# Transposes of the attention between single products of the projections instead of in runs

## The chip, the core and the metric

The kernel runs on one core of a Trainium2 chip. The metric is the time of one execution on the device, in microseconds (us). A core has a matrix engine (TensorE, PE in the profile, with its weight loads as PEld), three engines for elementwise work (VectorE or DVE, ScalarE or ACT, GpSimd or POOL) and a queue that issues transfers (SyncE or SP).

## The reference

One layer of a trunk for 512 tokens of width 1024, all in fp32. Three groups of attention heads share one input projection and one output projection; a gated MLP with a short convolution and a gated per-layer input follow.

```python
hn = rms_norm(h, ln_mix)
z = hn @ w_in                       # 1024 x 3590
(q1, q2, k1, k2, va, qf, kf, vf, fg, qc, kc, vc) = jnp.split(z, IN_SPLITS, axis=-1)
# A: differential attention, 4 heads:  softmax(q1 k1 + bias) - lam * softmax(q2 k2 + bias)
# B: forgetting attention, 6 heads:    bias from F = cumsum(log_sigmoid(fg + fgate_bias))
# C: chunked attention, 6 heads:       clipped relative-position bias
# q and k are RMS-normed for each head, head size 64
h = h + jnp.concatenate([o_a, o_b, o_c], axis=-1) @ w_out
h = h + conv_gated_mlp(rms_norm(h, ln_ffn), w_up, conv_w, conv_b, w_down)
gate = jax.nn.sigmoid(rms_norm(h, ln_ple) @ w_ple_gate)
h = h + (p @ w_ple_proj) * gate
```

## The kernel before

**Products.** Every fp32 operand is split into a high and a low part, and a product of two of them is three matmuls: high x high, high x low and low x high (`mm3`). A projection of 128 tokens has eight groups of three, one for each 128 rows of the weights; they add up in one PSUM bank, z. The columns are those of a pair of heads: `A0`, `A0b`, `A1`, `A1b` (two maps of two pairs of heads of A), `B0` to `B2`, `C0` to `C2`. For pairs of B and C, 384 columns are the q, k and v of two heads. The output projection (`wo`) has six groups of 512 columns.

**Attention.** For each pair of heads q and k come out of the projection with tokens in the partitions (`zn`). Four transposes for q and four for k (`feature_cols`, names `q_p` and `k_p`) put features in the partitions; ACT and DVE then split the results (`q_q`, `ql`, `k_k`, `kl`), and POOL moves halves together. Scores (`s`) follow, then the softmax on DVE, ACT and POOL (`e` and `st`). The probabilities are transposed as well (`prob_cols`): a run of four (`pt`), a run of three (`pt`) and a run of three (`ptc`) for each head; ACT and DVE split each (`pth`, `ptl`, `ptc`), and the products with the values (`po`) follow. `forget_cumsum` transposes the gates of B (`pf`), adds them up along the tokens with a scan on DVE (`fs`) and transposes the sums back (`pq`). A transpose is a matmul with a 128 x 128 identity as the moving operand (`ident` in the rows), in fp32. Its results go to one of three PSUM banks with the tag t; the z banks are two, and so are those for scores.

**Order of the work.** All of TensorE's order is written out by hand (`pe.pinned`). One slot is the projection of 128 tokens, or one block of the output projection. `run` goes through the eight groups of a slot, and behind each it lets one step of the attention issue its work: at first those that the table `T` names for this slot, from the group given there on. What is left at the slot's end is issued there in one go. A step issues one run of transposes, or one block of scores, or a pair of products with the values:

```python
for j in range(8):
    next(fill, None)
    while todo and j >= todo[0][0]:
        try:
            step(*todo[0][1:])
            break
        except StopIteration:
            todo.pop(0)
```

So before, a run of four transposes stands behind the third matmul of a group and ahead of the next group. On the attention's other engines the order isn't pinned: the scheduler of the framework sets it by priority (which follows the order in which the code issues the work, with the shifts of `EARLY`) and by its own model of time, when the program is built. Each engine then works in that order.

Nearly all instructions go through one recording helper, so they have the line L104 in the profile; they are told apart by their tiles. The rows leave out buffer numbers, and names of pairs are shortened: `A_`, `B_` and `C_` stand for any pair of the group. `B_l<-B_r,B_h` is a split of weights loaded ahead for a later projection.

Of the kernel before, what the change touches and what calls it, by code (L numbers as in the profile page):

```python
# [15 lines left out]
P = 128  # L16
D = 1024
S = 512
NT = S // P
KD = D // P  # L20
# [12 lines left out]
C_MIX, C_QK, C_SUB, C_CONV0, C_CONV1, C_CONV2, C_PLE, C_CONVB, C_FFN, C_FGB, C_LAM, NSMALL = (  # L33
    0, 8, 14, 16, 60, 104, 148, 156, 200, 208, 214, 470)
# [43 lines left out]
def kernel(ctx: ExitStack, tc: tile.TileContext, x, xt0, xt, pt_in, small, bias_c,  # L78
# [33 lines left out]
    pe, act, dve, pool, sp = (Engine(e) for e in (nc.tensor, nc.scalar, nc.vector, nc.gpsimd, nc.sync))  # L112
# [10 lines left out]
    Th = [cp.tile([P, 4, S], F32R, tag=f"Th{g}", name=f"Th{g}") for g in range(2)]  # L123
    Tl = [cp.tile([P, 4, S], F32R, tag=f"Tl{g}", name=f"Tl{g}") for g in range(2)]
# [12 lines left out]
    ident = cp.tile([P, P], F32, tag="ident", name="ident")  # L137
# [95 lines left out]
    def load_rect(w, k0, nk, c0, ncol, name, eng=dve, gain=None):  # L233
        rows = w[k0 * P : (k0 + nk) * P, c0 : c0 + ncol].rearrange("(k p) c -> p k c", p=P)
        return load_w(lambda raw: [(raw[:, : nk * ncol].rearrange("p (k c) -> p k c", k=nk), rows)],
                      nk, ncol, ncol, name, eng, gain)

    def mm3(acc, ah, al, bh, bl, first, last, **k):
        pe.matmul(acc, ah, bh, start=first, stop=False, **k)
        pe.matmul(acc, ah, bl, start=False, stop=False, **k)  # L240
        pe.matmul(acc, al, bh, start=False, stop=last, **k)
# [11 lines left out]
    def tcol(T, k, t):  # L253
        return T[k // 4][:, k % 4, t * P : (t + 1) * P]
# [51 lines left out]
    for b in range(2):  # L306
        for i in range(2):
            c = HALF[1 - i]
# [60 lines left out]
    gq = cp.tile([P, 8], F32, tag="gq", name="gq")  # L369
# [49 lines left out]
    def feature_cols(zn, j, name):  # L419
        pt = bank("t", f"{name}_p")  # L420
        for t in range(NT):
            pe.transpose(pt[:, t * P : (t + 1) * P], zn[:, t, j * P : (j + 1) * P], ident)
        return pt

    def move(dst, src):
# [1 line left out]

    def split_q(zn, g, name):

        pt = feature_cols(zn, 0, name)  # L430
        q0, q1 = (ap.tile([P, S], F32R, tag="q", bufs=4, name=f"{name}_q{i}") for i in range(2))
        lo = ap.tile([P, S], F32R, tag="ql", bufs=1, name=f"{name}_ql")
        act.activation(q0, pt, AF.Identity, scale=g)
        dve.scalar_tensor_tensor(lo, pt, g, f32(q0), ALU.mult, ALU.subtract)
        move(q1[DN], q0[DN])
        move(q0[DN], lo[UP])
        move(q1[UP], lo[DN])
        return q0, q1

    def split_k(zn, g, name):  # L440

        pt = feature_cols(zn, 1, name)
# [12 lines left out]
    V, QK, ZN = {}, {}, {}  # L455

    def project(ws, n, t, z, evac, prefetch):
        for k in range(KD):
            wh, wl = ws[k // 2]
            mm3(z[:, :n], tcol(Th, k, t), tcol(Tl, k, t), wh[:, k % 2, :], wl[:, k % 2, :], k == 0, k == KD - 1)  # L460
            if k < KD - 1:
                yield
        evac()
        for w in prefetch:
            w()
        yield
# [36 lines left out]
    def qk_cols(pr, part):  # L503
        need(*(("in", pr, part, t) for t in range(NT)))
        g = GAIN[pr[0]]
        zn = ZN[pr, part]
        q = split_q(zn, gq[:, g : g + 1], f"{pr}_q{part}")
        yield
        QK[pr, part] = (q, *split_k(zn, col(C_QK, g + 1), f"{pr}_k{part}"))
        yield  # L510


# [3 lines left out]
    def forget_cumsum():  # L516
        need(*(("in", "A0", 1, t) for t in range(NT)))
        xv = fg[:, :, 0:6]
        fa = ap.tile([P, NT, 6], F32, tag="fa", name="fa")
        dve.scalar_tensor_tensor(fa, xv, -1.0, xv, ALU.mult, ALU.max)  # L520
        act.activation(fa, fa, AF.Exp, scale=-1.0)
        act.activation(fa, fa, AF.Ln, bias=onec)
        dve.scalar_tensor_tensor(xv, xv, 0.0, fa, ALU.min, ALU.subtract)
        yield
# [10 lines left out]
        yield  # L535
        pq = bank("t", "pq")
        for t in range(NT):
            pe.transpose(pq[:, t * P : (t + 1) * P], fs[:, t * P : (t + 1) * P], ident)
        dve.tensor_copy(fq[:, :, 0:6], pq.rearrange("p (t c) -> p t c", t=NT)[:, :, 0:6])
        done("fc")  # L540
        yield
# [74 lines left out]
    def prob_cols(pr, hh):  # L616
        probs = PROB[pr, hh]
        tiles = []
        for kb in range(2):
            n = (NT - kb) * P  # L620
            pt = bank("t", f"{pr}_{hh}_pt{kb}")
            for qb in range(kb, NT):
                pe.transpose(pt[:, (qb - kb) * P : (qb - kb + 1) * P], probs[qb][:, kb * P : (kb + 1) * P], ident)
            th = ap.tile([P, S], F32R, tag="pth", bufs=3, name=f"{pr}_{hh}_pth{kb}")
# [4 lines left out]
            yield  # L629
        assert not PTC_OF  # L630
        PTC_OF.append((pr, hh))
        pt = bank("t", f"{pr}_{hh}_ptc")
        pe.transpose(pt[:, P : 2 * P], probs[3][:, 3 * P : 4 * P], ident)
        pe.transpose(pt[:, 2 * P : 3 * P], probs[2][:, 2 * P : 3 * P], ident)
        pe.transpose(pt[:, 3 * P : 4 * P], probs[3][:, 2 * P : 3 * P], ident)
# [67 lines left out]
    def out_unit(j, ks, wts, prefetch):  # L703

        acc = bank("zs"[j % 2] if ks[0] else "z", f"wo_{ks[0]}_{j}")
        c = slice(j % 4 * P, (j % 4 + 1) * P)
        for k in ks:
            wh, wl = (w[:, 0, c] for w in wts[k])
            mm3(acc, wh, wl, Th[k // 4][:, k % 4, :], Tl[k // 4][:, k % 4, :], k == ks[0], k == ks[-1])
# [14 lines left out]
    def step(early, g):  # L724
        if early:
            with tc.high_priority(offset=early):
                next(g)
        else:
            next(g)
# [21 lines left out]
    T = {  # L751
# [670 lines left out]
    sums, todo = None, ple_splits()  # L1422
# [282 lines left out]
    t = 0.0  # L1705
# [122 lines left out]
```

## Time and profile before

| | |
|---|---|
| three timed runs | 697.28 us median (695.9 to 697.84) |
| span of the profiled execution, first to last instruction | 692.9 us |
| granted clock of TensorE over the span | 1.000 |
| TensorE, busy | 678.8 us, 98% of the span |
| DVE, busy | 560.7 us, 81% |
| ACT, busy | 411.0 us, 59% |
| POOL, busy | 238.7 us, 34% |
| DMA | 133.84 MB, mean 193 GB/s |

The profiled execution has no time of its own beside its span; the median of the timed runs is 4.4 us above that span. Matmuls overlap in the profile: each is shown from its start to its modelled end, so the time that one takes of TensorE is the distance to the next start. In the rows of a timeline stand start, duration, engine, line, operation, out<-in, shapes and count; in brackets stands how long the engine was idle before and what released it. The attention lies between some 27 and 297 us, the up projection of the MLP starts at 308.88 us, and the last stage ends the span.

### The profile page before, as it was taken

The numbers are of one execution on the slowest core, as the hardware profiler recorded it, in microseconds if no ns is written. First come the engines' busy times: TensorE is split into PE (matmuls) and PEld (weight loads), VectorE is DVE, ScalarE is ACT, GpSimd is POOL, SyncE is SP. The second block draws the span as 40 slices with busy tenths as digits, with TensorE's granted clock in tenths as the row PEclk, the third lists the DMA queues.
The fourth block names the chain that finished last, engine by engine and source line by source line (L and its number), as shares of the span: only waits on it lengthen the run. The fifth ranks groups of instructions, "written<-read, shape, count | busy, mean of one in ns | idle before, by whom it ended". The sixth has DMA issues, their size and how long they took to land.

```text
span 692.9 us, 12202 instructions
## 1 busy us (share of the span) xinstructions
PE 678.8 (98%) x4244; PEld 617.7 (89%) x4244; DVE 560.7 (81%) x1168; ACT 411.0 (59%) x799; POOL 238.7 (34%) x349
## 2 busy tenths in 40 slices
PE   9999999999999999999999999999999999999997
PEld 8988989988999988878899899989998898999886
DVE  7678787888778875599788987898888889888863
ACT  7646766757656754475476655456664566556821
POOL 6586766757575540231211212211111210000210
PEclk9999999999999999999999999999999999999999
DMA  9554579746745174379999799998999884463441
GB/s 329 209 155 110 164 229 273 226 155 164 285 137 179 40 270 138 91 181 253 170 263 223 150 254 248 268 227 189 229 308 246 186 226 140 139 232 100 159 122 61
DMA packets 57112, 133.84 MB, mean 193 GB/s; under 512 B 6454, under 2 KB 8118, under 8 KB 57052
## 3 DMA queue, kind: packets, MB, share of 16 engines
q1 hardware_dynamic: 45660, 107.60, 47.3%
q0 software_dynamic: 11104, 25.17, 22.2%
q8 instruction: 33, 0.54, 0.3%
q10 hardware_dynamic: 288, 0.30, 0.1%
q14 instruction: 27, 0.22, 0.1%
HBM read 125.83 MB, written 44.05 MB: 245 GB/s over the span
## 4 chain that ended last, share of the span: by engine, by line
PE 83%; DVE 6%; POOL 3%; DMA 3%; ACT 2%; issue 2%; SPq 0%; POOLq 0%; DVEq 0%; ACTq 0%
PE u L104 22%; PE dn_X L104 9%; PE pg L104 6%; PE wo L104 6%; PE C_z L104 5%; PE sX L104 5%; PE dn_Y L104 4%; PE B_z L104 4%; PE sY L104 3%; PE sZ L104 3%; PE A_z L104 3%; PE dn_Z L104 2%; PE pp L104 2%; PE C_s L104 1%; DMA bias_B<-fk_d 1%
## 5 line engine op out<-in xcount | busy, mean ns | idle before, releaser
L104 DVE TENSOR_TENSOR w_lo<-w_raw,w_hi 128x768 fp32r<-128x768 f32 (+5 forms) x154 | 115.0, 786 | 9.4 <-ACT w_hi L104 9.2
L104 ACT CAST w_hi<-w_raw 128x768 fp32r<-128x768 f32 (+5 forms) x154 | 99.7, 687 | 33.8 <-PE dn_X L104 8.0
L104 PE MATMUL u<-Th,w_hi 128*128 128x512 f32 x224 | 87.0, 391 | 0.0
L104 PE MATMUL u<-Tl,w_hi 128*128 128x512 f32 x224 | 86.9, 390 | 0.0
L104 PE MATMUL u<-Th,w_lo 128*128 128x512 f32 x224 | 86.8, 390 | 0.0
L104 PEld LDWEIGHTS u<-Th,w_lo 128*128 128x128 f32 x224 | 42.0, 188 | 8.9
L104 PEld LDWEIGHTS u<-Th,w_hi 128*128 128x128 f32 x224 | 42.0, 188 | 8.6 <-ACT Th L104 0.4
L104 PEld LDWEIGHTS u<-Tl,w_hi 128*128 128x128 f32 x224 | 42.0, 188 | 8.1
L104 DVE SCALAR_TENSOR_TENSOR c<-u,cols,c 128x511 f32<-128x511 f32 (+1 forms) x56 | 41.0, 745 | 6.2 <-ACT c L104 5.7
L104 POOL DMA_DIRECT2D usum<-usum x16 | 13.0, 813 | 91.2 <-DMA usum<-in_w_up_dram 49.3
L104 PE MATMUL dn_X<-g_ah,w_hi 128*128 128x256 f32 x144 | 39.8, 276 | 0.0
L104 PE MATMUL dn_X<-g_ah,w_lo 128*128 128x256 f32 x144 | 39.8, 276 | 0.0
L104 PE MATMUL dn_X<-g_al,w_hi 128*128 128x256 f32 x144 | 39.8, 276 | 0.0
L104 PE MATMUL B_z<-B_h,Th 128*128 128x384 f32 x96 | 34.4, 358 | 0.7 <-DVE B_zn L104 0.6
L104 PE MATMUL C_z<-C_h,Th 128*128 128x384 f32 x96 | 34.3, 357 | 0.0
L104 PE MATMUL B_z<-B_h,Tl 128*128 128x384 f32 x96 | 32.3, 337 | 0.0
L104 PE MATMUL C_z<-C_h,Tl 128*128 128x384 f32 x96 | 32.3, 337 | 0.0
L104 PE MATMUL C_z<-C_l,Th 128*128 128x384 f32 x96 | 32.2, 336 | 0.0
L104 PE MATMUL B_z<-B_l,Th 128*128 128x384 f32 x96 | 32.2, 335 | 0.0
L104 POOL DMA_DIRECT2D dsum<-dsum x16 | 13.0, 814 | 53.5 <-DMA dsum<-dsum 24.5
L104 POOL TENSOR_TENSOR sums<-sums,n_sq 128x512 f32<-128x512 f32 x3 | 3.9, 1297 | 79.7 <-ACT n_sq L104 79.6
L104 ACT ACTIVATE c<-u,cols 128x512 f32<-128x512 f32 x28 | 21.5, 775 | 16.0 <-PE u L104 14.6
(504 smaller groups left out, 2385.4 us busy)
## 6 DMA issues: line engine op xcount, KB each, us to landing
w_raw<-in_w_up_dram SPq DMA_DIRECT2D x44, 384.0 KB, 6.9
dsum<-in_w_dsum_dram SPq DMA_DIRECT2D x12, 768.0 KB, 8.1
w_raw<-dsum SPq DMA_DIRECT2D x24, 384.0 KB, 5.9
usum<-in_w_usum_dram SPq DMA_DIRECT2D x32, 256.0 KB, 6.1
w_raw<-in_w_down_dram SPq DMA_DIRECT2D x18, 384.0 KB, 5.3
w_raw<-usum SPq DMA_DIRECT2D x16, 384.0 KB, 7.4
B_r<-in_w_in_dram SPq DMA_DIRECT2D x12, 384.0 KB, 3.7
C_r<-in_w_in_dram SPq DMA_DIRECT2D x12, 384.0 KB, 5.9
```

The costliest lines, as they stand in the source:

```text
L104: ins = getattr(self.eng, op)(*a, **k)
```

## The change

`run` now issues the transposes one at a time. The three matmuls of a group of a projection and the transposes of a run are generators that stop behind each instruction (`ONE`), and a run may start behind the second matmul of a group (`LEAD`); a unit that is about to start a run says so with `NEXT_COLS`. A unit's other steps are issued as before, behind a group. What is left at the end of a slot still comes out in one go, so some runs stay whole.

```diff
+    ONE, NEXT_COLS = "one", "cols"
+
+    def mm3_singly(acc, ah, al, bh, bl, first, last):
+        for i, (a, b) in enumerate(((ah, bh), (ah, bl), (al, bh))):
+            pe.matmul(acc, a, b, start=first and i == 0, stop=last and i == 2)
+            if i < 2:
+                yield ONE
...
         for t in range(NT):
             pe.transpose(pt[:, t * P : (t + 1) * P], zn[:, t, j * P : (j + 1) * P], ident)
+            if t < NT - 1:
+                yield ONE
         return pt
...
-            mm3(z[:, :n], tcol(Th, k, t), tcol(Tl, k, t), wh[:, k % 2, :], wl[:, k % 2, :], k == 0, k == KD - 1)
+            yield from mm3_singly(z[:, :n], tcol(Th, k, t), tcol(Tl, k, t), wh[:, k % 2, :], wl[:, k % 2, :], k == 0, k == KD - 1)
...
-        q = split_q(zn, gq[:, g : g + 1], f"{pr}_q{part}")
-        yield
-        QK[pr, part] = (q, *split_k(zn, col(C_QK, g + 1), f"{pr}_k{part}"))
+        q = yield from split_q(zn, gq[:, g : g + 1], f"{pr}_q{part}")
+        yield NEXT_COLS
+        k = yield from split_k(zn, col(C_QK, g + 1), f"{pr}_k{part}")
+        QK[pr, part] = (q, *k)
         yield
...
         for t in range(NT):
             pe.transpose(pf[:, t * P : (t + 1) * P], fg[:, t, :], ident)
+            if t < NT - 1:
+                yield ONE
...
             for qb in range(kb, NT):
                 pe.transpose(pt[:, (qb - kb) * P : (qb - kb + 1) * P], probs[qb][:, kb * P : (kb + 1) * P], ident)
+                if qb < NT - 1:
+                    yield ONE
...
+    FIRST_AT = {qk_cols: NEXT_COLS, prob_cols: NEXT_COLS}
+    LEAD = 2
+
+    class Unit:
+
+        def __init__(self, start, early, gen, args):
+            self.start, self.early, self.g, self.at = start, early, gen(*args), FIRST_AT.get(gen)
+
+        def go(self):
+            try:
+                self.at = step(self.early, self.g)
+            except StopIteration:
+                self.at = "end"
+            return self.at
 
     def run(fill, todo):
 
-        todo = [(start, early, gen(*args)) for start, early, gen, args in todo]
+        todo = [Unit(*q) for q in todo]
         for j in range(8):
-            next(fill, None)
-            while todo and j >= todo[0][0]:
-                try:
-                    step(*todo[0][1:])
+            busy = False
+            for i in range(3):
+                more = next(fill, None)
+                if todo and (todo[0].at == ONE or todo[0].at == NEXT_COLS and j >= todo[0].start and not busy and i >= 3 - LEAD and more == ONE):
+                    busy = todo[0].at != ONE or busy
+                    todo[0].go()
+                if more != ONE:
                     break
-                except StopIteration:
-                    todo.pop(0)
+            while not busy and todo and todo[0].at != ONE and j >= todo[0].start:
+                if todo[0].go() != "end":
+                    break
+                todo.pop(0)
         for _ in fill:
             pass
-        for _, early, g in todo:
-            try:
-                while True:
-                    step(early, g)
-            except StopIteration:
-                pass
+        for q in todo:
+            while q.at != "end":
+                q.go()
```

The output projection and the runs `pq` and `ptc` are changed in the same way. Of 248 transposes 59 were followed by something other than a transpose, and 178 are now.

On TensorE, the gates' transposes `pf` inside a projection of A (`A_z`), and `pq`, which read the scan's result; before:

```order
L104 MATMUL A_z_806<-A_3_l,Th_65 128x384
L104 MATMUL A_z_806<-A_3_h,Tl_67 128x384
L104 MATMUL pf<-ident,oall 128x128 x4
L104 MATMUL A_z_806<-A_3_h,Th_65 128x384
L104 MATMUL A_z_806<-A_3_l,Th_65 128x384
L104 MATMUL A_z_806<-A_3_h,Tl_67 128x384
L104 MATMUL pq<-ident,fs 128x128 x4
```

And now:

```order
L104 MATMUL A_z_806<-A_3_l,Th_65 128x384
L104 MATMUL pf<-ident,oall 128x128
L104 MATMUL A_z_806<-A_3_h,Tl_67 128x384
L104 MATMUL pf<-ident,oall 128x128
L104 MATMUL A_z_806<-A_3_h,Th_65 128x384
L104 MATMUL pf<-ident,oall 128x128
L104 MATMUL A_z_806<-A_3_l,Th_65 128x384
L104 MATMUL pf<-ident,oall 128x128
L104 MATMUL A_z_806<-A_3_h,Tl_67 128x384
L104 MATMUL pq<-ident,fs 128x128 x4
```

The first transpose stands one product earlier, the last one two products later, and one product instead of three is left between it and `pq`, which stay a run.

On DVE at the same place (`fs` is the scan, `A_0_3_e` the last update of a head's probabilities, `B_1_l` and `B_2_l` splits of weights, `nf` the sums that go to memory); what differs:

```order
 L104 TENSOR_TENSOR B_1_l<-B_1_r,B_1_h 128x768
-L104 SCALAR_TENSOR_TENSOR fs<-f_ones,pf 128x512
 L104 TENSOR_TENSOR B_2_l<-B_2_r,B_2_h 128x768
 L104 SCALAR_TENSOR_TENSOR A_0_3_e<-A_0_3_e,A_0_3_st,A_0_3b_e 128x512
+L104 SCALAR_TENSOR_TENSOR fs<-f_ones,pf 128x512
+L104 SCALAR_TENSOR_TENSOR A_V<-A_z_806,rstd,A_V 128x128
 L104 TENSOR_SCALAR nf<-fs 6x512
-L104 SCALAR_TENSOR_TENSOR A_V<-A_z_806,rstd,A_V 128x128
```

The scan moved behind a split and an update.

On DVE among the scores of the second pair of A, beside the first projections of B (`B_rs` the sums of squares, `B_zn` the normed q and k, after which a z bank is free); before:

```order
L104 ISA A_0_3b_e,A_0_3b_st<-A_0_3b_s,bias_A_1326 128x512
L104 ISA A_0_3b_st 128x1
L104 TENSOR_REDUCE B_rs_1392<-B_sq_1390 128x4
L104 RECIPROCAL A_0_3_st<-A_0_3_st 128x1
L104 SCALAR_TENSOR_TENSOR A_0_2_e<-A_0_2_e,A_0_2_st,A_0_2b_e 128x384
L104 TENSOR_TENSOR B_0_l<-B_0_r,B_0_h 128x768
L104 RECIPROCAL A_0_3b_st<-A_0_3b_st 128x1
L104 SCALAR_TENSOR_TENSOR B_zn<-B_z_1316,B_rs_1392 128x256
```

And now:

```order
L104 TENSOR_REDUCE B_rs_1392<-B_sq_1390 128x4
L104 RECIPROCAL A_0_2b_st<-A_0_2b_st 128x1
L104 ISA A_0_3b_e,A_0_3b_st<-A_0_3b_s,bias_A_1326 128x512
L104 ISA A_0_3b_st 128x1
L104 SCALAR_TENSOR_TENSOR A_0_1_e<-A_0_1_e,A_0_1_st,A_0_1b_e 128x256
L104 RECIPROCAL A_0_3_st<-A_0_3_st 128x1
L104 SCALAR_TENSOR_TENSOR A_0_2_e<-A_0_2_e,A_0_2_st,A_0_2b_e 128x384
L104 TENSOR_TENSOR B_0_l<-B_0_r,B_0_h 128x768
L104 SCALAR_TENSOR_TENSOR B_zn<-B_z_1316,B_rs_1392 128x256
```

The reduce moved ahead of the last score instruction and of an update, and `B_zn` ahead of a reciprocal.

More of the change, by code (lines that the diff above doesn't have):

```diff
@@ L428, in split_q @@
     def split_q(zn, g, name):
-        pt = feature_cols(zn, 0, name)
+        pt = yield from feature_cols(zn, 0, name)
         q0, q1 = (ap.tile([P, S], F32R, tag="q", bufs=4, name=f"{name}_q{i}") for i in range(2))
@@ L440, in split_k @@
     def split_k(zn, g, name):
-        pt = feature_cols(zn, 1, name)
+        pt = yield from feature_cols(zn, 1, name)
         k0, k1 = (ap.tile([P, S], F32R, tag="k", bufs=4, name=f"{name}_k{i}") for i in range(2))
@@ L523, in forget_cumsum @@
         dve.scalar_tensor_tensor(xv, xv, 0.0, fa, ALU.min, ALU.subtract)
-        yield
+        yield NEXT_COLS
         pf = bank("t", "pf")
@@ L534, in forget_cumsum @@
         nc.sync.dma_start(out=fk_d, in_=nf)
-        yield
+        yield NEXT_COLS
         pq = bank("t", "pq")
@@ L538, in forget_cumsum @@
             pe.transpose(pq[:, t * P : (t + 1) * P], fs[:, t * P : (t + 1) * P], ident)
+            if t < NT - 1:
+                yield ONE
         dve.tensor_copy(fq[:, :, 0:6], pq.rearrange("p (t c) -> p t c", t=NT)[:, :, 0:6])
@@ L623, in prob_cols @@
                 pe.transpose(pt[:, (qb - kb) * P : (qb - kb + 1) * P], probs[qb][:, kb * P : (kb + 1) * P], ident)
+                if qb < NT - 1:
+                    yield ONE
             th = ap.tile([P, S], F32R, tag="pth", bufs=3, name=f"{pr}_{hh}_pth{kb}")
@@ L628, in prob_cols @@
             tiles.append((th[:, :n], tl[:, :n]))
-            yield
+            yield NEXT_COLS
         assert not PTC_OF
@@ L632, in prob_cols @@
         pt = bank("t", f"{pr}_{hh}_ptc")
-        pe.transpose(pt[:, P : 2 * P], probs[3][:, 3 * P : 4 * P], ident)
-        pe.transpose(pt[:, 2 * P : 3 * P], probs[2][:, 2 * P : 3 * P], ident)
-        pe.transpose(pt[:, 3 * P : 4 * P], probs[3][:, 2 * P : 3 * P], ident)
+        for c, qb, kb in ((1, 3, 3), (2, 2, 2), (3, 3, 2)):
+            pe.transpose(pt[:, c * P : (c + 1) * P], probs[qb][:, kb * P : (kb + 1) * P], ident)
+            if c < 3:
+                yield ONE
         th, tl = ptc
@@ L708, in out_unit @@
             wh, wl = (w[:, 0, c] for w in wts[k])
-            mm3(acc, wh, wl, Th[k // 4][:, k % 4, :], Tl[k // 4][:, k % 4, :], k == ks[0], k == ks[-1])
+            yield from mm3_singly(acc, wh, wl, Th[k // 4][:, k % 4, :], Tl[k // 4][:, k % 4, :], k == ks[0], k == ks[-1])
             if k != ks[-1]:
@@ L726, in step @@
             with tc.high_priority(offset=early):
-                next(g)
-        else:
-            next(g)
+                return next(g)
+        return next(g)
+    FIRST_AT = {qk_cols: NEXT_COLS, prob_cols: NEXT_COLS}
[9 more added lines that the diff above has]
+            return self.at
     def run(fill, todo):
-        todo = [(start, early, gen(*args)) for start, early, gen, args in todo]
+        todo = [Unit(*q) for q in todo]
         for j in range(8):
-            next(fill, None)
-            while todo and j >= todo[0][0]:
-                try:
-                    step(*todo[0][1:])
+            busy = False
[5 more added lines that the diff above has]
+                if more != ONE:
                     break
-                except StopIteration:
-                    todo.pop(0)
+            while not busy and todo and todo[0].at != ONE and j >= todo[0].start:
+                if todo[0].go() != "end":
+                    break
+                todo.pop(0)
         for _ in fill:
             pass
-        for _, early, g in todo:
-            try:
-                while True:
-                    step(early, g)
-            except StopIteration:
-                pass
+        for q in todo:
+            while q.at != "end":
+                q.go()
     T = {
```

## The prediction

> **What bounds the kernel now.** I read the page first: the busy times, the clock row and the chain that ended last.
>
> ```profile
> span 692.9 us, 12202 instructions
> ...
> PE 678.8 (98%) x4244; PEld 617.7 (89%) x4244; DVE 560.7 (81%) x1168; ACT 411.0 (59%) x799; POOL 238.7 (34%) x349
> ...
> PEclk9999999999999999999999999999999999999999
> ...
> PE 83%; DVE 6%; POOL 3%; DMA 3%; ACT 2%; issue 2%; SPq 0%; POOLq 0%; DVEq 0%; ACTq 0%
> ```
>
> TensorE is the bound: 83% of the chain, at a full granted clock in every slice. DVE comes next. So the change can act in two ways only: a transpose and its neighbours take more or less of TensorE's time, or TensorE waits longer or shorter for something. The change lies in the attention, some 27 to 297 us of the span. I then read the timeline engine by engine around the runs of transposes. First a whole run on TensorE (PE) and its weight loads (PEld), and two rows of the chain of waits with matmuls of 512 columns (u) and 256 columns (sZ):
>
> ```profile
> 118.44 0.34 PE L104 MATMUL B_z<-B_h,Tl 128*128 128x384 f32 x1
> 118.62 0.60 PE L104 MATMUL B_q_p<-ident,B_zn 128*128 128x128 f32 x4
> 118.98 0.42 PE L104 MATMUL B_z<-B_h,Th 128*128 128x384 f32 x1
> 119.24 0.34 PE L104 MATMUL B_z<-B_l,Th 128*128 128x384 f32 x1
> 119.41 0.34 PE L104 MATMUL B_z<-B_h,Tl 128*128 128x384 f32 x1
> ...
> 118.44 0.54 PEld L104 LDWEIGHTS B_q_p<-ident,B_zn 128*128 128x128 f32 x4
> 118.95 0.19 PEld L104 LDWEIGHTS B_z<-B_h,Th 128*128 128x128 f32 x1
> ...
> 347.29 2.72 PE sZ L104 x24
> 354.09 6.83 PE u L104 x30
> ```
>
> Starts follow each other, durations overlap, so prices are differences of starts. A product of 384 columns costs 0.17 us (119.24 to 119.41). The run of four and one product fill 118.62 to 119.24, so the four cost 0.62 - 0.17 = 0.45 us, 0.11 us each. But width alone would make a transpose cheaper: 512 columns cost 6.83/30 = 0.228 us and 256 cost 2.72/24 = 0.113, so 128 columns come to 0.113 - 0.057 = 0.056 us. The other half is the weight load: the product's load starts only at 118.95, when the last transpose starts, and the product gets going at 119.24 - 0.17 = 119.07. One load is under way at a time, and a transpose is too short to cover the next one.
>
> **1. TensorE's own price of a break.** The programs hold 248 transposes in both versions. Before, a transpose is followed by something else 59 times, after it 178 times: 119 more breaks. A transpose behind a product has its own load covered, but now the product behind it has its load uncovered. From the fence: the first three transposes take 118.95 - 118.62 = 0.33 us, 0.11 each, the last one 119.07 - 118.95 = 0.12. So a break trades 0.11 for 0.12; the rows round to 0.01, so it costs between 0 and 0.01 us. I take the middle, 0.0055: 119 x 0.0055 = +0.65 us, ends 0 and +1.2. It is on the path, since TensorE is. If both loads were covered instead, each break would save 0.11 - 0.056 = 0.054, or 6.4 us in all; that is a rival below.
>
> The Trainium skill ("TensorE: Matmul & The Clock Gate", section "Step-by-step: what each phase is for") says that TensorE's queue pulls weight loads ahead of running matmuls, so that the next weights load under the present matmul. Read as any number of loads ahead it would give the 6.4 us; read as one load ahead it gives the rows above, where the load at 118.95 waited for the transpose before it.
>
> **2. The scan behind the first moved run of the gates.** The transposes `pf` feed the cumulative sum `fs` on DVE, which feeds the transposes `pq`; these stand as a run of four behind the next group of products in both versions. Here the order of DVE changes as well: `fs` falls behind the split B_2_l and the update A_0_3_e. PE, DVE and POOL there:
>
> ```profile
> 57.88 0.60 PE L104 MATMUL pf<-ident,oall 128*128 128x128 f32 x4
> ...
> 58.67 0.33 PE L104 MATMUL A_z<-A_h,Tl 128*128 128x384 f32 x1
> 59.93 0.66 PE L104 MATMUL pq<-ident,fs 128*128 128x128 f32 x4 [0.93 <-DVE fs L104]
> ...
> 57.79 0.96 DVE L104 TENSOR_TENSOR B_l<-B_r,B_h 128x768 fp32r<-128x768 f32 x1
> 58.66 1.21 DVE L104 TENSOR_TENSOR_SCAN fs<-f_ones,pf 128x512 f32<-128x512 f32 x1
> 59.79 0.93 DVE L104 TENSOR_TENSOR B_l<-B_r,B_h 128x768 fp32r<-128x768 f32 x1
> 60.64 1.10 DVE L104 SCALAR_TENSOR_TENSOR A_e<-A_e,A_st,A_3b_e 128x512 f32<-128x512 f32 x1
> 61.66 0.49 DVE L104 TENSOR_SCALAR nf<-fs 6x512 f32<-6x512 f32 x1
> ...
> 57.82 1.57 POOL L104 TENSOR_SCALAR A_3b_e<-A_3b_e,A_3b_st,nlam 128x512 f32<-128x512 f32 x1 [1.70 <-DVE A_3b_st L104]
> ```
>
> Before, `pf` ends, DVE is free at 58.66 and scans to 59.87, and TensorE waits 0.93 us at `pq`. Moving the last `pf` back by two products costs nothing in itself beyond 0.35 us of that wait; the order costs more. Behind the split (step 60.64 - 59.79 = 0.85) and the update (61.66 - 60.64 = 1.02) the scan starts 1.87 us later, in which the 0.35 is covered. The update's other input leaves POOL at 59.39, before DVE asks for it, so nothing more is added. Lower end: 0.35, if DVE's queue were empty by then; upper end: the full durations, 0.93 + 1.10 = 2.03. I take +1.75, near the steps, since the update overlapped with POOL work in this trace and may go a little faster. Queued behind `pq` on TensorE is every product of the stage; nothing behind it is waiting to be overtaken, so I let the delay stand to the end. The DMA of `nf` (SP's queue) goes out some 0.5 us later; its reader comes after `pq`'s delay anyway.
>
> **3. A shorter wait at the projection's bank.** About 100 us DVE's order changes the other way: the reduce of B's squares moves ahead of the last score instruction (A_0_3b_e), and B_zn ahead by one.
>
> ```profile
> 103.14 0.34 PE L104 MATMUL B_z<-B_h,Tl 128*128 128x384 f32 x1
> 104.09 0.41 PE L104 MATMUL B_z<-B_h,Th 128*128 128x384 f32 x1 [0.62 <-DVE B_zn L104]
> ...
> 99.81 0.67 DVE L104 CUSTOM_DVE_ANT_0 A_3b_e<-A_3b_s,bias_A 128x512 f32<-128x512 f32 x1
> ...
> 100.41 0.41 DVE L104 TENSOR_REDUCE B_rs<-B_sq 128x4 f32<-128x256 f32 x1
> ...
> 103.52 0.42 DVE L104 SCALAR_TENSOR_TENSOR B_zn<-B_z,B_rs 128x256 f32<-128x256 f32 x1 [1.17 <-POOL B_rs L104]
> ...
> 100.92 1.44 POOL L104 TENSOR_SCALAR B_rs<-B_rs,rstd 128x4 f32<-128x4 f32 x1 [0.19 <-DVE A_st L104]
> 102.45 1.04 POOL L104 TENSOR_TENSOR B_rs<-B_rs,nhalf 128x4 f32<-128x4 f32 x1
> ```
>
> TensorE starts a new projection at 104.09 instead of 103.14 + 0.17 = 103.31: 0.78 us waited for B_zn, which waited for POOL, which waited for the reduce. With the reduce 0.67 us or more earlier and POOL's first step ahead of another score scaling, most of this goes. I take -0.75; ends -0.78 - 0.2 (a score wait just behind it may go as well) and 0 (POOL's 1.44 us does not move).
>
> **4. Waits inside a run that now have work in them.** Three runs wait for their last inputs, and single products now stand in front of that wait instead of behind it. Rows of PE, POOL and DVE at the three places:
>
> ```profile
> 43.91 0.33 PE L104 MATMUL A_q_p<-ident,A0b_zn 128*128 128x128 f32 x1 [0.66 <-DVE A0b_zn L104]
> ...
> 47.45 2.00 POOL L104 TENSOR_SCALAR A_k_k<-A_k_k 64x512 fp32r<-64x512 f32 x3
> ...
> 49.51 0.39 PE L104 MATMUL A_0b_s<-A_k_k,A_q_q 128*128 128x256 f32 x1
> ...
> 167.84 0.33 PE L104 MATMUL B_q_p<-ident,B_zn 128*128 128x128 f32 x1 [0.42 <-DVE B_zn L104]
> ...
> 172.10 0.52 PE L104 MATMUL B_ptc<-ident,B_e 128*128 128x128 f32 x3
> ...
> 170.46 1.50 DVE L104 SCALAR_TENSOR_TENSOR kl<-B_k_p,cols,B_k_k 64x512 fp32r<-64x512 f32 x2
> 171.99 0.35 DVE L104 SCALAR_TENSOR_TENSOR C_V<-C_z,rstd,C_V 128x128 fp32r<-128x128 f32 x1
> ...
> 193.72 1.16 DVE L104 TENSOR_TENSOR B_ptl<-B_pt,B_pth 128x512 fp32r<-128x512 f32 x2
> 195.50 0.42 DVE L104 SCALAR_TENSOR_TENSOR C_zn<-C_z,C_rs 128x256 f32<-128x256 f32 x1 [0.63 <-POOL C_rs L104]
> ...
> 195.98 0.33 PE L104 MATMUL C_q_p<-ident,C_zn 128*128 128x128 f32 x1 [0.69 <-DVE C_zn L104]
> ...
> 196.67 0.60 PE L104 MATMUL C_k_p<-ident,C_zn 128*128 128x128 f32 x4
> ```
>
> At 43.91 two products (0.35 us) move into the wait. But the scores at 49.51 start just as POOL ends the keys (47.45 + 2.00 = 49.45), and that chain starts from the same transpose at 43.91: TensorE comes 0.35 us early and waits as long. Net 0. At 167.84 three products (0.52 us) move in, and the next wait takes them back: `ptc` needs the bank that DVE's pair `kl` frees (170.46 + 1.50 = 171.96), and DVE now does C_V (0.35) ahead of `kl`. Net +0.35; ends 0 and +0.5. At 195.98 again 0.52 us move in, but DVE now does C_zn ahead of the second half of B_ptl, whose bank the transposes C_k_p need: they may start at about 195.98 + 0.52 = 196.5, against 196.67. Net -0.15; ends -0.52 and +0.1.
>
> **5. Later last transposes elsewhere.** In the other moved runs the last transpose comes two to three products (0.35 to 0.52 us) later, its readers on ACT and DVE mostly find those engines busy, and the matmuls that need the result stand a microsecond or more behind. I cost them at 0; the cover is that distance, and where it is gone a wait of up to 0.35 us appears at the values' matmuls.
>
> **The sum**, against the profiled execution: 0.65 + 1.75 - 0.75 + 0 + 0.35 - 0.15 = +1.85, of which I round down 0.2 for waits just behind item 3: +1.65 us. Its span of 692.9 us becomes 694.5. The median of the three runs shown is 697.28, 4.4 us above that span and outside what the edit touches, so the time is 698.9 us. A difference under 0.3%, 2.1 us, is about what a measurement here cannot tell from no change; 699.4 is the border.
>
> **The rivals.**
> - *The scan's delay stays and nothing is given back* (slower). Place: `pq` at 59.93. Price: up to 2.03 there, 0.65 for the breaks, 0.35 - 0.15 from item 4, with the wait at 104.09 unchanged: +2.9, 700.2 us. It decides as soon as less than 0.3 us of the 0.78 at 104.09 is returned. For it: POOL's 1.44 us step may be what holds B_zn. Against it: the reduce does move ahead of 0.67 us of DVE work.
> - *The delay at `pq` is made up* (no change). TensorE is late by 1.75 us at 62 us, but later waits, 0.78 at 104.09 among them, could shrink with it if what they wait for does not hang on TensorE. Then 0.65 + 0.35 - 0.15 - 0.95 remain, or -0.1, and at most half the delay on top: 697.2 us, up to 698.1. Against it: in that stage DVE mostly waits for TensorE's scores.
> - *The loads are hidden* (faster). Each break saves 0.054 us: -6.4, and with the +1.0 of the other items -5.4: 691.9 us. For it: no transpose stands alone between products in this trace, so the load behind one that comes after a product was never seen. Against it: the product's load starts at 118.95, with the last transpose, and not before. This is the wide reading of the skill's rule above.
>
> **How the numbers follow.** Forecast 0.45 (697.9 to 699.9 by its ends, a fifth of it over the border), full delay 0.30, made up 0.18, hidden loads 0.07. So faster 0.07; slower 0.30 + 0.08 = 0.38; the same 0.55. The range leaves out the hidden loads and the outermost ends: 696.7 to 701.0 us.
>
> **What would show it.** TensorE's wait at `pq` near 2.8 us instead of 0.93, with the scan behind B_l and A_e on DVE. Interleaved transposes at 0.11 to 0.12 us from their start to the next product's real start; at 0.06 the third rival holds. The wait at 104 us gone or under 0.2. The wait inside C_q_p gone, and a short one before C_k_p. The prediction is wrong if the span from 300 us on changes: nothing there is touched. It is also wrong if new waits of several tenths stand before the values' matmuls (B_po, C_po), which I cost at nothing.

## The result, and the profile after

The changed kernel took 700.59 us (median of 4 executions, 699.63 to 701.11); the kernel before, beside it, 697.21 us (4 executions, 695.9 to 697.84). The ratio is 1.0056, with a 95% interval of 1.0039 to 1.0073. A later group, again with both kernels side by side, gave 699.32 us (6 executions) against 695.83 us (23), ratio 1.0047, 1.0032 to 1.0062. So the change costs about half a per cent. The forecast was 698.9 us and "about the same": the time lies inside its range (696.7 to 701.0), but the change is slower by more than the 0.3% that was named as the border.

The lines of the page that answer to those of before:

```profile
span 699.3 us, 12201 instructions
...
PE 682.4 (98%) x4244; PEld 620.0 (89%) x4244; DVE 561.8 (80%) x1168; ACT 409.5 (59%) x799; POOL 235.1 (34%) x349
...
PEclk9998999999999999999999999999999999999999
...
PE 83%; DVE 6%; DMA 4%; POOL 3%; issue 2%; ACT 1%; SPq 0%; POOLq 0%; DVEq 0%; ACTq 0%
```

Look at the clock row: one 8 in the fourth of 40 slices, 52 to 70 us. Before, every slice had a 9. Nothing else in these lines stands out against before. The profiled execution took 701.11 us, so 1.8 us of a time lie outside the span; in the other executions it is 1.7 to 1.8 us. The prediction had put 4.4 us there: the profiled execution of before (span 692.9 us) was some 2.6 us shorter than the median of the runs shown. The two spans, 6.4 us apart, therefore overstate the change, and medians are compared below.

The same stretch as in the prediction, of the changed kernel: TensorE first, then VectorE, then POOL. Columns are start, duration, engine, line, operation, output and inputs, and in brackets the idle time ahead and what ended it:

```profile
58.27 0.27 PE L104 MATMUL pf<-ident,oall 128*128 128x128 f32 x1
58.30 0.42 PE L104 MATMUL A_z<-A_h,Tl 128*128 128x384 f32 x1
...
59.14 0.27 PE L104 MATMUL pf<-ident,oall 128*128 128x128 f32 x1
59.16 0.42 PE L104 MATMUL A_z<-A_h,Tl 128*128 128x384 f32 x1
62.71 1.11 PE L104 MATMUL pq<-ident,fs 128*128 128x128 f32 x4 [3.13 <-DVE fs L104]
63.48 0.56 PE L104 MATMUL A1b_z<-A1b_h,Th 128*128 128x256 f32 x1
63.84 0.41 PE L104 MATMUL A1b_z<-A1b_l,Th 128*128 128x256 f32 x1
64.05 0.41 PE L104 MATMUL A1b_z<-A1b_h,Tl 128*128 128x256 f32 x1
```

```profile
58.35 1.83 DVE L104 TENSOR_TENSOR B_l<-B_r,B_h 128x768 fp32r<-128x768 f32 x2
60.77 0.75 DVE L104 SCALAR_TENSOR_TENSOR A_e<-A_e,A_st,A_3b_e 128x512 f32<-128x512 f32 x1 [0.59 <-POOL A_3b_e L104]
61.44 1.21 DVE L104 TENSOR_TENSOR_SCAN fs<-f_ones,pf 128x512 f32<-128x512 f32 x1
```

```profile
56.02 0.67 POOL L104 TENSOR_SCALAR A_2b_e<-A_2b_e,A_2b_st,nlam 128x384 f32<-128x384 f32 x1
58.38 2.36 POOL L104 TENSOR_SCALAR A_3b_e<-A_3b_e,A_3b_st,nlam 128x512 f32<-128x512 f32 x1 [1.70 <-DVE A_3b_st L104]
```

The scan `fs` comes behind two splits and `A_e`, as forecast. But `A_e` itself waits 0.59 us for POOL, whose step takes 2.36 us here and took 1.57 before. The wait at `pq` is 3.13 us instead of 0.93. And behind it the products of 256 columns follow each other every 0.21 us (63.84 to 64.05), where 256 columns cost 0.113 in the prediction's rows. The windows of the same trace say why (stretch, its length, TensorE's busy time and count, weight loads, VectorE, ScalarE, POOL, then the granted clock, DMA share and GB/s):

```profile
60.00:63.00 3.00, 0.29 (x2) 0.29 (x3) 2.41 (x5) 1.22 (x4) 1.86 (x3) 0.82 0.89 281
63.00:66.00 3.00, 3.00 (x16) 3.00 (x15) 1.15 (x3) 0.31 (x1) 2.40 (x6) 0.50 0.86 196
66.00:69.00 3.00, 3.00 (x17) 3.00 (x16) 1.11 (x2) 0.63 (x2) 0.91 (x3) 0.54 0.51 159
69.00:72.00 3.00, 3.00 (x25) 2.87 (x24) 1.55 (x4) 1.86 (x4) 0.12 (x1) 1.00 0.48 147
```

While TensorE stood idle its granted clock went to one half, and came back near 68.8 us. None of the prediction's steps had this. Of the four executions, the three with a granted clock of 0.993 or 0.994 over the span, this one among them, took 700.52 to 701.11 us; the one with 0.997 took 699.63. Of the waits further on (the list by place: total, times, longest), these differ most from before; the wait of 0.62 us for B_zn near 104 us and that of 0.69 us inside C_q_p are gone from the list:

```profile
PE B_s L104 <- DVE B_st L104: 1.3, 3, 0.5
PE B_s L104 <- POOL B_k_k L104: 1.0, 1, 1.0
...
PE B_ptc L104 <- DVE kl L104: 0.7, 1, 0.7
```

### The profile page after: what moved, and what is told of

Read it like the earlier page. It is cut to its first block, busy times and chain, and to the rows that moved or that the text cites. A ratio compares the mean times of both kernels' runs of the same rounds, so it can differ in the third digit from the quotient of the medians.

```text
span 699.3 us, 12201 instructions
## 1 busy us (share of the span) xinstructions
PE 682.4 (98%) x4244; PEld 620.0 (89%) x4244; DVE 561.8 (80%) x1168; ACT 409.5 (59%) x799; POOL 235.1 (34%) x349
## 4 chain that ended last, share of the span: by engine, by line
PE 83%; DVE 6%; DMA 4%; POOL 3%; issue 2%; ACT 1%; SPq 0%; POOLq 0%; DVEq 0%; ACTq 0%
PE u L104 22%; PE dn_X L104 9%; PE pg L104 6%; PE wo L104 6%; PE C_z L104 6%; PE B_z L104 5%; PE sX L104 5%; PE dn_Y L104 4%; PE sY L104 3%; PE sZ L104 3%; PE dn_Z L104 2%; PE A1b_z L104 2%; PE pp L104 2%; DMA h<-in_x_dram 1%; DMA waq<-in_w_in_dram 1%
## 5 line engine op out<-in xcount | busy, mean ns | idle before, releaser
L104 PE MATMUL B_z<-B_h,Tl 128*128 128x384 f32 x96 | 34.4, 358 | 0.0
L104 PE MATMUL C_z<-C_h,Tl 128*128 128x384 f32 x96 | 33.9, 353 | 0.0
L104 PE MATMUL B_z<-B_l,Th 128*128 128x384 f32 x96 | 33.8, 352 | 0.0
L104 PE MATMUL C_z<-C_l,Th 128*128 128x384 f32 x96 | 33.6, 350 | 0.0
```

The source lines that it names most:

```text
L104: ins = getattr(self.eng, op)(*a, **k)
```

## The experiments

The theory after the result: the loss sits at `pq`, as some 2.2 us of longer wait and then the halved clock; the rest of the change nets out near zero. Rival 1: each of the 119 breaks costs 0.03 us. Rival 2: the small new waits from 145 us on make the loss.

**The change taken apart at the gates.** Two kernels complement each other: the changed kernel with `pf` as a run again (and `pq`, which stands as a run either way), and the kernel before with `pf` alone issued singly. With them ran the kernel before, unchanged.

```diff
 e1_pf_as_a_run: in the changed kernel
-        yield NEXT_COLS
+        yield
         pf = bank("t", "pf")
         for t in range(NT):
             pe.transpose(pf[:, t * P : (t + 1) * P], fg[:, t, :], ident)
-            if t < NT - 1:
-                yield ONE
 e2_pf_alone: these lines kept; those of feature_cols, qk_cols and prob_cols undone
```

> The changed kernel with one thing undone: the transposes pf of the gates stand as a run of four again, so that the scan fs is back ahead of B_2_l and A_0_3_e on VectorE; all other transposes stay single (116 of the 119 breaks remain). Theory (the loss sits at pq: 2.2 us more wait there and 2.7 us of halved clock behind it): wait at pq back to about 0.9 us, granted clock 1.00 from 60 to 69 us, time 697.2 us, between 696.3 and 698.0. Rival 1 (each break costs some 0.03 us, 119 of them make the 3.4 us): 700.5 us, the wait at pq shorter but nothing gained. Rival 2 (the small new waits from 145 to 205 us make the loss): 699.5 to 700.5 us.

> The kernel before with one thing done: only the transposes pf of the gates are issued singly (3 of the 119 breaks), everything else in runs as before. On VectorE the scan fs moves behind B_2_l and A_0_3_e. Theory: the whole loss is there, wait at pq near 3 us and the clock at 0.5 to 0.8 for some 6 us behind it, time 697.2 + 3.5 to 5 = 700.7 to 702.2 us. Rivals 1 and 2: the wait grows but the total stays within 697 to 698 us, since three breaks cost 0.1 us and the later stage is in the order of before.

> The kernel before, unchanged, to see the clock and the span of each of its executions beside the profiled one (span 692.9 us, clock 1.000). Theory: 697.2 us, and the executions longer than the profiled one show a granted clock a little under 1.000, or waits at the same places that are longer by a few tenths. If all show 1.000 and 695.4 us of span, the profiled execution was shorter for another reason, to be read from the second trace.

Before took 695.99 us in this group (24 executions). Taken a second time as a run of its own, it gave 696.48 us (12 executions), ratio 1.0012 (0.9998 to 1.0025): the same kernel against itself, so a ratio that near to 1 tells nothing. With `pf` as a run: 696.64 us, ratio 1.0008 (0.9993 to 1.0023). With `pf` alone: 699.86 us, ratio 1.0060 (1.0042 to 1.0078). So three breaks make a loss as large as the whole change, and the other 116 make at most 0.2%. That refutes both rivals, which had the first of these at 699.5 to 700.5 us. `pq` in the one, then in the other with its three windows (TensorE alone, clock behind its count):

```profile
60.97 0.66 PE L104 MATMUL pq<-ident,fs 128*128 128x128 f32 x4 [0.93 <-DVE fs L104]
```

```profile
63.14 0.47 PE L104 MATMUL pq<-ident,fs 128*128 128x128 f32 x1 [3.08 <-DVE fs L104]
```

```profile
60.00:63.00 3.00, 0.06 (x1) 0.96 0.85 258
63.00:66.00 3.00, 2.86 (x14) 0.50 0.94 238
66.00:69.00 3.00, 3.00 (x25) 0.97 0.38 109
```

The second trace of before has a span of 693.4 us and a clock of 1.00 through 60 to 72 us. Its `pq` waits 0.93 us too; its executions run from 695.11 to 699.55 us. The expectation that longer executions show a lower clock held only loosely: executions of 697 us stood at a clock of 0.996 to 1.000, and no trace shows where those with 0.996 lost it.

**The wait filled.** Constant matmuls ahead of `pq`, into the bank that `pq` overwrites, keep TensorE busy without moving anything else. Three amounts were tried, with the changed kernel again beside the second.

```diff
         pq = bank("t", "pq")
+        for _ in range(24):        # e3; 8 in e5_fill_a_third, 14 in e10_fill_half
+            pe.matmul(pq[:, 0 : 2 * P], wt.broadcast_to([P, P]), wt.broadcast_to([P, 2 * P]), start=True, stop=True)
```

> The changed kernel with 24 bf16 matmuls of 256 columns on constants (about 0.11 us each, 2.6 us) added ahead of pq, into pq's bank, which pq then overwrites; all orders around pq stay. They fill the wait for the scan fs with work, so TensorE does not stand idle, while pq still starts when fs is there. Theory (idle time brings the clock down, which costs 2.7 us on top of the wait): granted clock 1.00 from 60 to 69 us, time 700.6 - 2.7 = 697.9 us, 697.3 to 698.8. If the wait alone costs and the clock does not: 700.6 us, or a little more. Rivals 1 and 2: 700.6 us.

> The changed kernel, unchanged, on the chip and beside the kernels of this group, to compare them without another chip between. Theory: 1.0056 of before, wait at pq 3.1 us, and a low clock behind it that lasts either about 3.4 us (as in the kernel with pf alone) or about 6.8 us (as in the profiled execution of the changed kernel), so that its executions spread by some 1.7 us. If the clock is 1.00 behind pq, the halved clock was an accident of one execution.

> The changed kernel with only 8 of the constant matmuls ahead of pq (0.95 us of work at the start of the wait), which leaves some 2.2 us of idle time. Theory (the clock comes down behind idle time of about 3 us, not 2): granted clock 1.00 behind pq, ratio as with 24 of them, 1.0036 (1.002 to 1.005). If 2.2 us of idle time are enough to bring the clock down: ratio 1.0056, as without filling.

> The changed kernel with 14 of the constant matmuls ahead of pq, some 1.6 us of work, which leaves about 1.5 us of idle time: between the 0.9 us that left the clock alone and the 2.2 us that brought it down. If the length of the idle time decides, with a border near 2 us, the clock stays at 1.00 behind pq; if a border is nearer to 1 us, it halves for 3.4 us and the time is that of the changed kernel.

Rows of `pq` and the window behind it, with 24, 8 and 14 of them:

```profile
60.13 2.86 PE L104 MATMUL pq<-const-bfloat16-1.0 128*128 128x256 bf16 x24
63.41 0.65 PE L104 MATMUL pq<-ident,fs 128*128 128x128 f32 x4 [0.42 <-DVE fs L104]
```

```profile
63.00:66.00 3.00, 2.58 (x23) 1.00 0.98 251
```

```profile
63.23 1.12 PE L104 MATMUL pq<-ident,fs 128*128 128x128 f32 x4 [2.23 <-DVE fs L104]
```

```profile
63.00:66.00 3.00, 2.77 (x13) 0.52 0.97 242
66.00:69.00 3.00, 3.00 (x25) 0.92 0.40 118
```

```profile
62.46 0.66 PE L104 MATMUL pq<-ident,fs 128*128 128x128 f32 x4 [1.55 <-DVE fs L104]
```

```profile
63.00:66.00 3.00, 3.00 (x29) 1.00 0.78 172
```

With 0.42 us or 1.55 us of idle time the clock stays at 1.00 and the ratios are 1.0036 (1.0022 to 1.0050) and 1.0031 (1.0017 to 1.0045). With 2.23 us it halves in the profiled execution, and the ratio is 1.0047 (1.0032 to 1.0063), the same as the changed kernel's 1.0047 beside it. My border of 3 us was wrong, and the length of the wait alone is not what decides. By its records in the 14 traces, the granted clock changes on a grid: each stretch between two changes lasts a multiple of 3.413 us. From the first rise to the fall it is 58.03 us, 17 steps, in all four traces that halve here. What differs is how the wait lies on this grid (idle time is the step's length less TensorE's busy time):

| trace | step with the wait, us | idle in it, us | clock in the next step, idle in it | clock in the one after |
|---|---|---|---|---|
| 14 matmuls | 60.00 to 63.41 | 1.55 | 1.00, 0.00 us | 1.00 |
| 8 matmuls | 59.68 to 63.09 | 2.09 | 0.50, 0.14 us | 1.00 |
| `pf` alone | 59.37 to 62.78 | 2.72 | 0.50, 0.36 us | 1.00 |
| changed kernel, 2nd | 58.49 to 61.91 | 2.55 | 0.50, 0.58 us | 1.00 |
| changed kernel, 1st | 58.52 to 61.93 | 2.35 | 0.50, 0.78 us | 0.50 |

Over all steps of the 14 traces that began at full clock and lie within the span, the clock fell behind every one with 1.95 us of idle time or more, and behind none with 1.85 us or less; those nearest the border stand at the program's end. The last row also says why the clock once stayed low for two steps, though that is a single case. And the same wait need not halve the clock each time: three of the six executions with 8 matmuls, and one of the changed kernel's six in that group, have a clock of 0.999 or 1.000 over the span, where one low step of 3.4 us alone would leave 0.998 (1 - 0.5 x 3.4 / 698).

The expected gain of 2.7 us was too large as well: 0.11 to 0.16 per cent are 0.8 to 1.1 us, and the intervals of filled and unfilled overlap, so the clock's share of the time is seen in the traces and not shown by the medians. In the second trace of the changed kernel the clock was low for 3.4 us, not 6.8:

```profile
60.00:63.00 3.00, 0.51 (x3) 0.82 0.90 272
63.00:66.00 3.00, 3.00 (x18) 0.61 0.75 163
66.00:69.00 3.00, 3.00 (x25) 1.00 0.40 94
```

A window's clock of 0.82 over 3 us means 3 x 0.18 / 0.5 = 1.1 us at one half; 0.61 means 2.3 us. The sum is 3.4 us here, 3.4 us with `pf` alone (0.2 + 3.0 + 0.2), and 6.8 us in the first trace (1.1 + 3.0 + 2.8). Of that, the part behind the start of `pq` costs half its length: 1.5 us with `pf` alone, 3.0 us in the first trace.

**The wait removed.** If `pq`'s wait is path time, taking it away should pay even in the kernel before. There `pq` was moved three groups of products later; in the changed kernel the same, with `pf`, still single, one group earlier.

```diff
-        yield                          # ahead of pq, at the end of forget_cumsum
+        X["fs"] = fs
+        yield
+    def forget_rows():                 # the rest of forget_cumsum, a unit of its own
+        fs = X["fs"]
 ...
+        "fr": (12, 2),                 # its slot; e7_single_no_wait also: "fc": (11, 4), was (11, 5)
```

> The kernel before with one move: the run of four transposes pq stands three groups of products later, at the next projection, so that TensorE has 1.1 us of products to do while VectorE scans. Theory (TensorE's wait at pq is path time, one to one): the wait of 0.93 us is gone and the time falls by 0.9 us, ratio 0.9987 (0.997 to 1.000). Rival (the time is given back at the transposes of the probabilities behind, which wait for VectorE): ratio 1.000.

> The changed kernel with the gates' work moved: the transposes pf, still single, start one group of products earlier, so that the scan stands ahead of B_2_l and A_0_3_e on VectorE again, and pq stands three groups later as in the kernel before. All transposes but pq are single. Theory: no wait at pq, clock 1.00, time 3.4 + 0.9 us under the changed kernel, so that only the breaks (0.65 us) and the small waits are left against before: ratio 0.9995 (0.998 to 1.001). Rival 1 (each break costs 0.03 us): ratio 1.004. Rival 2 (the small waits from 145 us on): ratio 1.003 to 1.005.

The kernel before with a later `pq` took 696.25 us, ratio 1.0011 (0.9998 to 1.0023): nothing gained. The rival was right. `pq` no longer waits, but three others do:

```profile
60.98 0.66 PE L104 MATMUL pq<-ident,fs 128*128 128x128 f32 x4
...
62.85 0.33 PE L104 MATMUL A_pt<-ident,A_e 128*128 128x128 f32 x1 [0.52 <-DVE A_e L104]
66.89 0.38 PE L104 MATMUL A1b_z<-A1b_h,Th 128*128 128x256 f32 x1 [0.26 <-DVE A_zn L104]
...
70.41 0.39 PE L104 MATMUL A_1b_s<-A_k_k,A_q_q 128*128 128x256 f32 x1 [0.42 <-DVE A_0b_st L104]
```

Counted as in the table below, TensorE is ahead by 0.3 us at the first A_po and late by 1.0 us at 98.6 us. For the first of the three waits the reason is plain: A_e leaves VectorE 3.9 us after `pf` starts in both kernels, and before, the wait at `pq` covered this. The other two stand behind an order of VectorE that has changed by then, and were not tried apart. The changed kernel so mended took 697.39 us, ratio 1.0015 (1.0004 to 1.0026): 177 of 178 breaks and no wait at `pq`. Rival 1's 1.004 is excluded once more.

**The rest by kind of transpose.** In e8 only those of queries and keys are single, in e9 only those of the probabilities (`yield ONE` dropped in the other functions, `FIRST_AT` cut to the one unit). In e11 only one unit of the former is single:

```diff
+    def single(name):
+        pr, part = name[:2], int(name[-1])
+        return (pr, part) == ("A1", 1)
 ...
-            if t < NT - 1:
+            if t < NT - 1 and single(name):
                 yield ONE
```

> Only the transposes of the queries and keys are issued singly (42 of the 119 breaks); the gates' and the probabilities' stand in runs as before. On VectorE this has the reduce of B's squares ahead of A_0_3b_e near 104 us, and C_V ahead of kl at the second B pair. Theory (the waits move, one by one, and a break costs 0.0055 us): +0.25 for the breaks, -0.8 to -1.0 at 104 us, +0.4 at ptc, -0.3 at C_q_p: -0.5 us, ratio 0.999 (0.997 to 1.001). Rival 1 (a break costs 0.03 us): +1.3 us, ratio 1.002.

> Only the transposes of the probabilities are issued singly (74 of the 119 breaks); the gates' and those of the queries and keys stand in runs as before. The waits at 104 us, ptc and C_q_p should stand as before, and the score waits on B_st near 155 us grow by 0.6 us. Theory: +0.4 for the breaks and +0.6 at B_st: +1.0 us, ratio 1.0014 (1.000 to 1.003). Rival 1 (a break costs 0.03 us): +2.2 us, ratio 1.003.

> Only the transposes of one unit, the second queries and keys of A1 (A_q_p and A_k_p from A1b_zn, near 88 to 90 us), are issued singly: 6 of the 119 breaks. The order on VectorE, POOL and ScalarE differs from before only between 86 and 107 us, and there in all that item 3 named (the reduce of B's squares ahead of A_0_3b_e, B_zn earlier). Theory: the wait of 0.78 us at 104 us goes, half a microsecond of it is left behind the scores as in the kernel with the queries and keys alone, and what came later there (1.3 us at C_V, 0.4 us at ptc) does not come: 0.5 to 0.9 us under before, ratio 0.999 (0.9975 to 1.000). Rival: the gain of 0.16 per cent in the kernel with the queries and keys alone had another place; then the ratio is 1.000.

Queries and keys alone: 695.34 us against 696.23, ratio 0.9984 (0.9971 to 0.9996), the only version whose interval lies below 1, by little more than the 0.12% by which the same kernel differed from itself. Probabilities alone: 697.51 us, ratio 1.0019 (1.0007 to 1.0030). The one unit: 695.70 against 695.87 us, ratio 0.9998 (0.9984 to 1.0011), so the expected 0.5 to 0.9 us did not show. New waits of the three, in their order:

```profile
191.00 0.41 PE L104 MATMUL C_z<-C_h,Th 128*128 128x384 f32 x1 [1.32 <-ACT C_V L104]
```

```profile
70.37 0.44 PE L104 MATMUL A_s<-A_k_k,A_q_q 128*128 128x384 f32 x1 [0.26 <-DVE A_st L104]
...
156.73 0.47 PE L104 MATMUL B_s<-B_k_k,B_q_q 128*128 128x512 f32 x1 [0.37 <-DVE B_st L104]
```

```profile
189.70 0.41 PE L104 MATMUL C_z<-C_h,Th 128*128 128x384 f32 x1 [0.72 <-DVE C_zn L104]
```

TensorE's delay along the program shows where each trace gains and loses. It is counted from the first transpose of `pf`: the start of the named matmul minus that start, in each trace, minus the same in the second trace of before (us; its own times stand in the first column). In e2, e3 and both traces of after, `pf` starts one product earlier, and 0.17 us of each of their figures is that alone.

| at | before, 1st | e1 | e2 | e3 | after, 1st | after, 2nd | e8 | e9 | e11 |
|---|---|---|---|---|---|---|---|---|---|
| 65.1, first A_po | 0.0 | 0.0 | 3.7 | 2.4 | 5.2 | 3.7 | 0.0 | 0.0 | 0.0 |
| 98.6, A_s | 0.2 | 0.8 | 3.6 | 2.8 | 5.3 | 3.9 | 0.2 | 0.7 | 0.1 |
| 110.3, A_s | 0.2 | 0.2 | 3.7 | 2.1 | 4.6 | 3.2 | -0.5 | 0.7 | -0.6 |
| 143.2, second B_po | 0.2 | 0.5 | 3.6 | 2.5 | 5.0 | 3.5 | -0.5 | 1.0 | -0.6 |
| 173.4, B_po | 0.7 | 2.4 | 4.7 | 3.9 | 6.9 | 5.7 | 0.9 | 2.6 | -0.7 |
| end | 0.6 | 1.8 | 4.4 | 2.9 | 6.6 | 5.3 | 1.9 | 2.3 | 0.2 |

Two traces of before differ by 0.6 us at the end, so a difference of that size between columns says nothing. What is beyond it: the jump at the gates, in e2 and both traces of after; the fall between 98.6 and 110.3 us, 0.6 to 0.7 us wherever queries and keys are single and none elsewhere; and the rise from 143 to 173 us. That rise has three parts: up to 1.1 us of waiting for POOL's B_k_k near 146 us, which comes and goes between executions of one kernel; 0.4 us at `ptc`, with queries and keys; and 0.6 us of score waits on B_st, with the probabilities.

## Why the prediction was wrong, point by point

- *A break costs 0 to 0.01 us*: right. In the trace after, three pairs of a transpose and a product of 384 columns take 59.14 - 58.27 = 0.87 us, 0.29 each, less 0.174 for the product: 0.116 against 0.11 in a run. Across the program, 116 breaks with all else that moves leave e1 at a ratio of 1.0008. The weight loads are not hidden; that rival falls.
- *The scan's delay, +1.75 us with an upper end of 2.03*: this step failed, twice. First the wait grew by 2.2 us (3.13 against 0.93). The sentence "The update's other input leaves POOL at 59.39, before DVE asks for it, so nothing more is added" took POOL's 1.57 us as fixed. In the eight traces of this study with the scan ahead of the second split it is 1.54 to 1.58 us; in the six with the scan behind both, 2.33 to 2.36. The trace of before could have told it, for there the same step of the second pair runs with nothing beside it on VectorE:

```profile
105.31 0.78 POOL L104 TENSOR_SCALAR A_3b_e<-A_3b_e,A_3b_st,nlam 128x512 f32<-128x512 f32 x1
```

One split beside it makes 1.57, that is 0.79 more, so two make 2.36. The Trainium skill ("GPSIMD Engine Reference", section "1. Specifications") says that GpSimd shares its SBUF interfaces with VectorE and contends with instructions that have two SBUF inputs; the splits have two, and the trace agrees. Second, the idle time brought the clock down, for which the prediction had no term: another 1.5 or 3.0 us by the length of the low clock. By the first row of the table, less the 0.17 us, it is 1.3 and 2.8 us: e2 is late by 3.5 us there and the first trace of after by 5.0, while e3, with the same wait filled, is late by 2.2. So the term should have been about 3.5 us or more; e2, which changes nothing else, is late by 3.9 us in the medians.
- *The sum*: with 3.5 in place of 1.75 it is 3.4 us, and 3.4 us were measured (700.59 - 697.21). That the rest nets out as forecast is luck, for two more of its terms did not hold: the gain at 104 us and the 0 for later last transposes, below. In the chances, a fifth of 0.45 is 0.09 and not 0.08, which moves nothing.
- *The delay stays to the end*: right, by e2's column from 65 to 143 us.
- *104 us, -0.75*: right in place and size (0.7 us between 98.6 and 110.3 us in e8 and e11, 0.7 in both traces after), but it is no gain at the end: in the trace of e11 it is given back at C's projections by 190 us.
- *Waits inside runs*: the second pair's `ptc` costs what was forecast (0.69 us of wait, forecast +0.35 net; e8 rises by 0.4 there). The wait inside C_q_p is gone, and a short one of 0.13 us stands before C_k_p, as forecast. At 43.91 the net is 0, as forecast: the wait is 0.48 us instead of 0.66, and one of 0.20 us has come at 50.07.
- *Later last transposes elsewhere, 0*: wrong. With the probabilities alone the time rises by 1.3 us (ratio 1.0019, 1.0007 to 1.0030), of which the breaks' term makes 0.4. But the waits did not come where the prediction would have had them, at the values' matmuls (the wait of a B_po near 142 us is 0.23 us and was 0.26): they are waits of the scores for VectorE, at 70 and 157 us. How a late transpose leads there was not followed.
- *The rivals*: "the scan's delay stays and nothing is given back" came nearest in time (700.2), but by other sums: more was lost at `pq`, and the wait at 104 us did go.
- *Nothing changes from 300 us on*: right, to 0.3 us in both traces of after.

Two things stay open. Whether the 0.16% of e8 is a gain, and from where, is not shown: it is not the wait at 104 us alone, and its profiled execution (696.46 us) was slower than its median. And POOL's B_k_k, for which the scores near 146 us wait 0.55 us in the first trace of before, not at all in the second, and about 1 us in most others, stands behind a load (`bias_B`) whose landing differs between executions. It was not tried apart.

## What to carry to other kernels

Before a wait is moved or lengthened, ask what the longer idle time does to the clock: here a stall of 3.1 us cost up to 3 us more behind it by the traces, and filling half of it with throwaway matmuls kept the clock up. When a small edit lets a scheduler reorder another engine, price the new neighbours too: an instruction's duration in the trace holds beside the instructions that ran with it then. And a wait that goes away on the bound engine pays only if the engine it waited for has time to spare; otherwise it turns up at the next meeting, as in e6 and in the trace of e11.

## What the runs showed of the hardware

The granted clock changed on a grid of 3.41 us. It fell to one half behind steps of this grid in which TensorE was idle for 1.95 us or more, behind none with 1.85 us or less, and stayed low for 3.4 us or 6.8 us, even with TensorE busy. The Trainium skill ("TensorE: Matmul & The Clock Gate", section "Part 1: The HAM clock gate (the "warmup" mystery)") tells of a free-running window of about 3.4 us, after at least one idle one of which the clock halves, and after a busy one of which it returns. The grid agrees with that window, and one and two windows are what the low stretches measure. But with 8 matmuls the window ahead of the fall was idle for 2.09 us only, so a wholly idle window is not needed; the measurement decides.

A POOL step of 128 x 512 took 0.78 us alone, 1.54 to 1.58 us beside one of VectorE's splits of 128 x 768 and 2.33 to 2.36 us beside two.
